# Turning attention probabilities with VectorE and a trip through DRAM instead of TensorE transposes

## Chip, core and metric

The kernel runs on one core of one Trainium2 chip. The metric is device time in microseconds (us) of one execution. Before the change the median of three runs is 538.23 us (538.05 to 538.24).

## What is computed

One layer of a decoder block for 256 tokens of 1024 features, in float32. A SwiGLU feed-forward network with 2816 hidden features comes first and another comes last; between them stands a mixing layer with two branches, attention with 8 heads of 64 features and a gated linear mixing of positions in chunks of 128 (gMLP). Cut to what matters here:

```python
def reference(x, ...):
    h = x + 0.5 * swiglu(rmsnorm(x, ffn1_norm), ffn1_w_gate, ffn1_w_up, ffn1_w_down)
    n = rmsnorm(h, mix_norm)
    z = n @ w_in                                   # q, k, v and both halves of the gMLP
    attn = moba_attention(q, k, v)                 # 256 tokens are one block: causal softmax attention
    gm = u * (tril(w_s) @ layernorm(v_gmlp) + b_s) # chunks of 128
    gates = sigmoid(n @ w_gate + b_gate)           # 2 x 1024 gates
    merged = gates[:, :D] * (attn @ w_branch_attn) + gates[:, D:] * (gm @ w_branch_gmlp)
    h = h + merged @ w_out
    h = h + 0.5 * swiglu(rmsnorm(h, ffn2_norm), ffn2_w_gate, ffn2_w_up, ffn2_w_down)
    return rmsnorm(h, final_norm)
```

For a head, the softmax gives probabilities with queries along the rows and keys along the columns. The product with the values sums over keys. TensorE sums over partitions, so the probabilities are needed with the keys on the partitions: they have to be transposed.

## The kernel before

**Weights.** All weights pass through one stream of units. A unit is fetched in two halves of 512 KB by the SyncE (SP) queue into one of 7 buffers `raw` (L137), and each half is split into a rounded high part (ScalarE, ACT, L212) and a remainder (VectorE, DVE, L214) in one of 4 unit buffers `w`; TensorE (PE) multiplies with three products in place of one. A fetch waits until the half that was in its buffer seven halves earlier has been split. In the stretch of the change the units are named `gate` (8), then `ba` and `bg` (the two branch projections, taken in turn), then `out`.

**Order.** PE and SP run in the order in which the code is written. DVE and ACT are ordered by a scheduler, except in blocks that say otherwise. PSUM has eight banks, taken in turn.

**The mixing stage.** After q, k and u (the names `pq`, `pu`) PE computes the scores (`sc`, L586) and the mixing of positions (`mix`, L571). DVE masks the scores and finds maxima, ACT takes exponentials (L601), DVE scales by the reciprocal sums (L604, L606). Probabilities stand in `prob`: 128 queries by 8 heads by 128 keys for the first 128 tokens, and by 256 keys for the second. Meanwhile PE computes 16 blocks of gates, `pgate` (L162 and L167; 24 matmuls each), by the loop at L666. `collect` (L205, L209) takes each out of PSUM; DVE and ACT finish it. With four of the blocks goes `gated`, which finishes the gMLP branch and frees the banks of `mix`.

**The transposes.** Behind block 7 `turn(0)` issues 12 transposes by PE (`pk`, L634 to L636), which ACT and DVE copy out (`pT`, L640, L642). Behind block 10 the products with the values of the first four heads follow (`attend`, names `po`, L651 and L653), and then `turn(2)`, the 12 transposes of the other heads; behind block 13 come the last four heads' products. Their result `ao` is then multiplied with the branch weights (`pb`).

**A transfer of the same kind.** In the second feed-forward network the hidden state is turned in the same way as the change will do it: DVE transposes it in squares of 32 (L715), four DMAs of 256 KB write it to DRAM from 32 partitions each in rows of 1 KB (`hd`, L723), and two DMAs of 512 KB bring it back (`ht`, L727).

Of the kernel before, what the change touches and what calls it, by code (L numbers as in the profile page):

```python
# [10 lines left out]
F32 = mybir.dt.float32  # L11
# [7 lines left out]
P = 128  # L19
D = 1024  # L20
S = 256
NT = S // P
DFF = 2816
KB = D // P
FB = DFF // P
HEADS = 8
HD = 64
# [16 lines left out]
def block_kernel(ctx, tc, t, out):  # L44
    nc = tc.nc
# [4 lines left out]
    act = ctx.enter_context(tc.tile_pool(name="act", bufs=1))  # L50
    tmp = ctx.enter_context(tc.tile_pool(name="tmp", bufs=2))
    small = ctx.enter_context(tc.tile_pool(name="small", bufs=4))
    psum = ctx.enter_context(tc.tile_pool(name="psum", bufs=8, space=PSUM))
    dram = ctx.enter_context(tc.tile_pool(name="dram", bufs=1, space=bass.MemoryType.DRAM))

    def bank(name):
        return psum.tile([P, 512], F32, tag="ps", name=name)
# [3 lines left out]
    h = act.tile([P, KB, S], F32, tag="h", name="h")  # L61
# [15 lines left out]
    ident = consts.tile([P, P], F32, name="ident")  # L77
# [133 lines left out]
    def split(hi, lo, src, later=False):  # L211
        nc.scalar.copy(hi, src)  # L212
        def rest():
            nc.vector.tensor_sub(lo, src, hi.bitcast(F32))  # L214
        return rest if later else rest()

    def alloc_T(name, tags):

        return [act.tile([P, 4, 2, S], F32R, tag=tag, name=f"{name}{c}") for c, tag in enumerate(tags)]
# [170 lines left out]
    def products(i0, nT, name, f, gu=None, ahead=ALONE):  # L390
        if gu is None:
            gu = tmp.tile([P, 2, S], F32, tag="gu", name=f"gu{name}{f}")
        w = unit(i0 + f, ahead)
        ps = [bank(f"{name}{'gu'[i]}{f}") for i in range(2)]
        by_passes([(ps[i], weights_of(w, nT, i)) for i in range(2)])
        for i in range(2):
            collect(gu[:, i, :], ps[i])
        return gu
# [50 lines left out]
    first = act.tile([P, 4, 2, S], F32, tag="nD", name="first")  # L449
# [3 lines left out]
    ps = {(f, i): bank(f"f1_{f}{i}") for f, i in at}  # L453
# [59 lines left out]
    with in_order():  # L513
# [6 lines left out]
        mix_a, mix_b = mixed[:, :FB], mixed[:, FB:]  # L520
        gates = mix_a[:, :2 * KB, :]
        gv = mix_a[:, 2 * KB:2 * KB + 4, :].rearrange("p (j a) t -> p j (a t)", j=NT)
        va = mix_b[:, 0:4, :].rearrange("p (j a) t -> p j (a t)", j=NT)
# [5 lines left out]
        prob = [mix_b[:, 8:12, :].rearrange("p a (b n) -> p (a b) n", b=2), mix_b[:, 12:20, :]]  # L529
# [36 lines left out]
    def spatial(ps, gp):  # L566

        for j in range(NT):
            for a in range(2):
                g = 2 * gp + a  # L570
                nc.tensor.matmul(ps[a * HD:(a + 1) * HD, j * P:(j + 1) * P],  # L571
                                 gv[:, j, g * HD:(g + 1) * HD], wsT[:, g, :], start=True, stop=True)


    for j in range(NT):
        n = (j + 1) * P
        per = 512 // n
        pr = prob[j]
        pr2 = pr.rearrange("p (a two) n -> p a two n", two=2)
        for a0 in range(0, HEADS // 2, per):  # L580

            pair = [bank(f"sc{j}{a0}{two}") for two in range(2)]
            for a in range(per):
                for two in range(2):
                    r = slice(two * HD, (two + 1) * HD)
                    nc.tensor.matmul(pair[two][:, a * n:(a + 1) * n], qT[r, a0 + a, j * P:(j + 1) * P],  # L586
                                     kT[r, a0 + a, :n], start=True, stop=True)
            for two in range(2):
                ps = pair[two].rearrange("p (a n) -> p a n", a=per)
                to = pr2[:, a0:a0 + per, two, :]  # L590
                if j:
                    nc.scalar.copy(to[:, :, :n - P], ps[:, :, :n - P])
                nc.vector.tensor_add(to[:, :, n - P:], ps[:, :, n - P:],
                                     mask[:, None, :].to_broadcast([P, per, P]))
        mx = small.tile([P, HEADS], F32, tag="mx", name=f"mx{j}")
        nc.vector.tensor_reduce(mx, pr, axis=AX.X, op=ALU.max)
        nm = small.tile([P, HEADS], F32, tag="nm", name=f"nm{j}")
        nc.vector.tensor_scalar(nm, mx, -(HD ** -0.5), None, op0=ALU.mult)
        sm = small.tile([P, HEADS], F32, tag="sm", name=f"sm{j}")
        for hd in range(HEADS):  # L600
            nc.scalar.activation(pr[:, hd, :], pr[:, hd, :], AF.Exp, bias=nm[:, hd:hd + 1],  # L601
                                 scale=HD ** -0.5, accum_out=sm[:, hd:hd + 1])
        ri = small.tile([P, HEADS], F32, tag="ri", name=f"ri{j}")
        nc.vector.reciprocal(ri, sm)  # L604
        for hd in range(HEADS):
            nc.vector.tensor_scalar(pr[:, hd, :], pr[:, hd, :], ri[:, hd:hd + 1], None, op0=ALU.mult)  # L606


    mix = []
    for pair in range(2):  # L610
        ps = bank(f"mix{pair}")
        for q in range(2):
            mix.append(ps[:, q * S:(q + 1) * S])
            spatial(mix[-1], 2 * pair + q)

    def gate_block(f):
        gz = tmp.tile([P, S], F32, tag="s", name=f"gz{f}")
        collect(gz, by_weights(f"pgate{f}", mg + f // 2, nT2, f % 2))  # L620
        nc.vector.tensor_mul(gz, gz, rows2)
        nc.scalar.activation(gates[:, f, :], gz, AF.Sigmoid, bias=bgate[:, f:f + 1])

    aoT, gmT = alloc_T("ag", ("nC", "nD"))

    def turn(first):

        hps = range(first, first + 2)
        pk0, pk1 = [bank(f"pk0{hp}") for hp in hps], bank(f"pk1{first}")
        for hp in hps:  # L630
            for a in range(2):
                hd, c1 = 2 * hp + a, (2 * (hp - first) + a) * P
                ps = pk0[hp - first]
                nc.tensor.transpose(ps[:, a * S:a * S + P], prob[0][:, hd, :], ident)  # L634
                nc.tensor.transpose(ps[:, a * S + P:a * S + S], prob[1][:, hd, :P], ident)
                nc.tensor.transpose(pk1[:, c1:c1 + P], prob[1][:, hd, P:], ident)  # L636
        t0 = []
        for hp, ps in zip(hps, pk0):
            t0.append(tmp.tile([P, 512], F32, tag="hg", name=f"pT0{hp}"))
            nc.scalar.copy(t0[-1], ps)  # L640
        t1 = tmp.tile([P, 512], F32, tag="gu", name=f"pT1{first}")
        nc.vector.tensor_copy(t1, pk1)  # L642
        return {hp: (t0[q], t1[:, q * S:(q + 1) * S]) for q, hp in enumerate(hps)}

    def attend(hp, t0, t1):

        po = bank(f"po{hp}")
        for a in range(2):
            hd = 2 * hp + a
            r = slice(a * HD, (a + 1) * HD)  # L650
            nc.tensor.matmul(po[r, :S], va[:, 0, hd * HD:(hd + 1) * HD], t0[:, a * S:(a + 1) * S],  # L651
                             start=True, stop=False)
            nc.tensor.matmul(po[r, P:S], va[:, 1, hd * HD:(hd + 1) * HD], t1[:, a * P:(a + 1) * P],  # L653
                             start=False, stop=True)
        split(aoT[:, hp, 0, :], aoT[:, hp, 1, :], po[:, :S])

    def gated(gp):
        m = tmp.tile([P, NT, P], F32, tag="s", name=f"mixb{gp}")
        nc.vector.tensor_add(m, mix[gp].rearrange("p (j i) -> p j i", j=NT),
                             bs[:, gp:gp + 1, :].to_broadcast([P, NT, P]))  # L660
        m2 = tmp.tile([P, S], F32, tag="us", name=f"gm{gp}")
        nc.vector.tensor_mul(m2, m.rearrange("p j i -> p (j i)"), uT[:, gp, :])
        split(gmT[:, gp, 0, :], gmT[:, gp, 1, :], m2)


    for f in range(2 * KB):  # L666
        gate_block(f)
        if f < 4:
            gated(f)
        if f == 7:  # L670
            turned = turn(0)
        elif f == 10:
            for hp in range(2):
                attend(hp, *turned[hp])
            turned = turn(2)
        elif f == 13:
            for hp in range(2, 4):
                attend(hp, *turned[hp])


    mT = alloc_T("mg", ("nA", "nB"))
    for f in range(KB):
        i = mb + 2 * (f // 4)
        ps = bank(f"pb{f}")
        c = slice(f % 4 * P, (f % 4 + 1) * P)
# [14 lines left out]
    with in_order():  # L700
# [3 lines left out]
        first = act.tile([P, 3, 2, S], F32, tag="nA", name="first2")  # L704
        gu = [products(f2, nT3, "f2", f, first[:, f]) for f in range(2)]
# [11 lines left out]
    hd = dram.tile([S, D], F32, name="hd")  # L717
# [117 lines left out]
```

## Time and profile before

| | |
|---|---|
| median of the runs | 538.23 us |
| the profiled execution: its time, its span | 538.72 us, 536.8 us |
| PE busy (matmul) | 528.8 us, 98% of the span |
| PE weight loads | 463.5 us, 86% |
| DVE busy | 405.9 us, 76% |
| ACT busy | 303.0 us, 56% |
| share of the SP queue's packets on 16 DMA engines | 58.2% |
| mean granted PE clock | 0.996 |

The span runs from the first to the last instruction. The profiled execution is 0.49 us above the median. A row of the timeline has the start in us from the span's start, the duration in us (of the whole row, where it holds several instructions), the engine, line, operation, what is written and read, the shape and the count; in brackets stands idle time before it and what ended that. A row of SPq is the issue of a transfer, not its duration.

### The profile page before, as it was taken

How to read it: one execution, taken by the hardware profiler on the slowest of the kernel's cores; microseconds unless marked ns; L12 is line 12 of the kernel's file. 1: busy time of each engine (PE TensorE's matmuls, PEld its weight loads, DVE VectorE, ACT ScalarE, POOL GpSimd, SP SyncE). 2: the span in 40 equal slices, each digit the busy share in tenths (PEclk: the TensorE clock that was granted, in tenths of full speed). 3: DMA queues.
4: the chain of work that ended last, by engine and by line, in shares of the span. 5: the costliest groups of instructions: out<-in, count | busy, mean ns of one | idle time of the engine just before them, and what ended most of it. 6: DMA issues, size and time to landing. Idle time of an engine off the chain costs nothing.

```text
span 536.8 us, 8141 instructions
## 1 busy us (share of the span) xinstructions
PE 528.8 (98%) x3049; PEld 463.5 (86%) x3049; DVE 405.9 (76%) x682; ACT 303.0 (56%) x534; POOL 17.7 (3%) x23
## 2 busy tenths in 40 slices
PE   8999999999999999999999999999999999999995
PEld 7888888888888888888888998888888888888884
DVE  6799998788443689978897787799898878854324
ACT  7768566565433367447886544476657656553402
POOL 0040000000000001000000000001000000000002
PEclk9999999999999999999999999999999999999998
DMA  8985765657756329764266545259588765565002
GB/s 319 396 286 178 253 224 187 197 195 218 230 170 203 103 86 322 258 210 147 80 196 203 172 135 182 96 174 315 165 268 292 235 197 197 178 214 177 20 1 79
DMA packets 31287, 104.10 MB, mean 194 GB/s; under 512 B 3472, under 2 KB 6032, under 8 KB 31248
## 3 DMA queue, kind: packets, MB, share of 16 engines
q1 hardware_dynamic: 30960, 103.25, 58.2%
q8 instruction: 24, 0.39, 0.3%
q10 hardware_dynamic: 288, 0.33, 0.2%
q14 instruction: 15, 0.12, 0.1%
HBM read 101.47 MB, written 2.10 MB: 193 GB/s over the span
## 4 chain that ended last, share of the span: by engine, by line
PE 97%; DMA 1%; DVE 0%; issue 0%; ACT 0%; POOLq 0%; DVEq 0%; POOL 0%; ACTq 0%
PE acc L162 10%; PE f2u L162 7%; PE f2g L162 7%; PE f1u L162 7%; PE f1g L162 7%; PE pgate L162 6%; PE acc L167 5%; PE f2u L167 4%; PE f2g L167 4%; PE f1u L167 4%; PE f1g L167 4%; PE acch L200 4%; PE acch L198 4%; PE acch L199 4%; PE pgate L167 3%; PE pq L162 3%
## 5 line engine op out<-in xcount | busy, mean ns | idle before, releaser
L214 DVE TENSOR_TENSOR w<-raw,w 128x1024 fp32r<-128x1024 f32 x180 | 219.3, 1238 | 53.4 <-ACT w L212 53.0
L212 ACT CAST w<-raw 128x1024 fp32r<-128x1024 f32 x180 | 181.8, 1057 | 59.3 <-PE acc L167 21.2
L162 PE MATMUL f2g<-n,w 128*128 128x512 f32 x176 | 68.8, 391 | 0.0
L162 PE MATMUL f2u<-n,w 128*128 128x512 f32 x176 | 68.8, 391 | 0.0
L162 PE MATMUL f1g<-n,w 128*128 128x512 f32 x160 | 62.6, 391 | 0.0
L162 PE MATMUL f1u<-n,w 128*128 128x512 f32 x160 | 62.5, 391 | 0.0
L162 PE MATMUL acc<-f1h,w 128*128 128x512 f32 x176 | 43.4, 391 | 0.0
L167 PE MATMUL f2u<-n,w 128*128 128x256 f32 x176 | 43.2, 283 | 0.0
L167 PE MATMUL f2g<-n,w 128*128 128x256 f32 x176 | 43.0, 282 | 0.0
L167 PE MATMUL f1u<-n,w 128*128 128x256 f32 x160 | 39.2, 283 | 0.0
L167 PE MATMUL f1g<-n,w 128*128 128x256 f32 x160 | 39.1, 282 | 0.0
L162 PEld LDWEIGHTS f2u<-n,w 128*128 128x128 f32 x176 | 33.1, 188 | 6.3
L162 PEld LDWEIGHTS f2g<-n,w 128*128 128x128 f32 x176 | 33.1, 188 | 6.1
L162 PEld LDWEIGHTS acc<-f1h,w 128*128 128x128 f32 x176 | 31.9, 188 | 5.8
L162 PEld LDWEIGHTS f1u<-n,w 128*128 128x128 f32 x160 | 30.1, 188 | 5.7
L162 PEld LDWEIGHTS f1g<-n,w 128*128 128x128 f32 x160 | 30.1, 188 | 5.6
L167 PEld LDWEIGHTS f2u<-n,w 128*128 128x128 f32 x176 | 33.7, 191 | 0.9
L167 PEld LDWEIGHTS f2g<-n,w 128*128 128x128 f32 x176 | 33.6, 191 | 0.9
L162 PE MATMUL pgate<-n,w 128*128 128x512 f32 x128 | 33.1, 396 | 0.0
L199 PE MATMUL acch<-w,f2h 128*128 128x512 f32 x84 | 32.7, 389 | 0.0
L200 PE MATMUL acch<-w,f2h 128*128 128x512 f32 x84 | 32.7, 389 | 0.0
L198 PE MATMUL acch<-w,f2h 128*128 128x512 f32 x84 | 32.7, 389 | 0.0
(191 smaller groups left out, 933.0 us busy)
## 6 DMA issues: line engine op xcount, KB each, us to landing
raw<-in_f SPq DMA_DIRECT2D x84, 512.0 KB, 5.1
raw<-in_f1d SPq DMA_DIRECT2D x22, 512.0 KB, 4.4
raw<-in_f2d SPq DMA_DIRECT2D x22, 512.0 KB, 3.9
raw<-in_gate SPq DMA_DIRECT2D x16, 512.0 KB, 4.6
raw<-in_qk SPq DMA_DIRECT2D x8, 512.0 KB, 5.4
raw<-in_out SPq DMA_DIRECT2D x8, 512.0 KB, 4.4
front<-in_first SPq DMA_DIRECT2D x7, 384.0 KB, 5.9
raw<-in_v SPq DMA_DIRECT2D x4, 512.0 KB, 4.5
```

The lines of the kernel that those rows point to most:

```text
L162: nc.tensor.matmul(ps, st, both.rearrange("p two n -> p (two n)"), start=first, stop=last)
L167: nc.tensor.matmul(ps[:, n:], st, both[:, 0, :], start=False, stop=False)
L198: nc.tensor.matmul(ps, sh, mh, start=first, stop=False)
L199: nc.tensor.matmul(ps, sh, ml, start=False, stop=False)
L200: nc.tensor.matmul(ps, sl, mh, start=False, stop=last)
L212: nc.scalar.copy(hi, src)
L214: nc.vector.tensor_sub(lo, src, hi.bitcast(F32))
```

## The change

The probabilities are no longer transposed by PE. When a block of queries has been scaled, DVE transposes it in squares of 32 by 32 into `turned` (4 instructions for the first 128 queries, 8 for the others). Eight DMAs on the SP queue (`to_keys`) write these to DRAM, in rows of 1 KB, so that each key gets its row: four of 128 KB behind gate block 2, four of 256 KB behind block 4. Three more of 512 KB (`by_keys`), behind block 6, bring them back with the keys on the partitions, over the place where the probabilities were. All products with the values follow behind block 10, where only half of them were. The copies out of PSUM fall away, `mix` is written ahead of the softmax in the code, and the attention result has a tile of its own.

```diff
+    turned = []
     for j in range(NT):
...
             nc.vector.tensor_scalar(pr[:, hd, :], pr[:, hd, :], ri[:, hd:hd + 1], None, op0=ALU.mult)
...
+        turned.append(mix_a[:, 2 * KB:2 * KB + 4, :] if j == 0 else
+                      act.tile([P, KB, S], F32, tag="nC", name="turned1"))
+        for kb in range(n // 32):
+            nc.vector.transpose(turned[j][:, kb, :].rearrange("p (h c) -> p h c", c=32),
+                                pr[:, :, kb * 32:(kb + 1) * 32])
...
-    def turn(first):
...
+    on_way = [dram.tile([(j + 1) * P, 4, S], F32, name=f"on_way{j}") for j in range(NT)]
+
+    def to_keys(j):
+        for b in range(4):
+            nc.sync.dma_start(on_way[j][:, b, :].rearrange("(k r) n -> r k n", r=32),
+                              turned[j][32 * b:32 * (b + 1)])
+
+    def by_keys():
+        for j, t0, b0 in ((0, 0, 8), (1, 0, 12), (1, 1, 16)):
+            nc.sync.dma_start(mix_b[:, b0:b0 + 4, :], on_way[j][t0 * P:(t0 + 1) * P])
...
-            nc.tensor.matmul(po[r, :S], va[:, 0, hd * HD:(hd + 1) * HD], t0[:, a * S:(a + 1) * S],
+            nc.tensor.matmul(po[r, :S], va[:, 0, hd * HD:(hd + 1) * HD], mix_b[:, 8:16, c],
                              start=True, stop=False)
-            nc.tensor.matmul(po[r, P:S], va[:, 1, hd * HD:(hd + 1) * HD], t1[:, a * P:(a + 1) * P],
+            nc.tensor.matmul(po[r, P:S], va[:, 1, hd * HD:(hd + 1) * HD], mix_b[:, 16:20, c],
                              start=False, stop=True)
...
-        if f == 7:
-            turned = turn(0)
+        if f in (2, 4):
+            to_keys(f // 2 - 1)
+        elif f == 6:
+            by_keys()
         elif f == 10:
-            for hp in range(2):
-                attend(hp, *turned[hp])
-            turned = turn(2)
-        elif f == 13:
-            for hp in range(2, 4):
-                attend(hp, *turned[hp])
+            aoT, = alloc_T("ao", ("nC",))
+            for hp in range(4):
+                attend(hp)
```

Where this puts the transfers on the SP queue is shown by the order in which it issues them. `raw` is a buffer of fetched weights. Before, around the first half of the first `bg` unit:

```order
L137 DMA raw_0_2687<-in_ba 128x1024
L137 DMA raw_1_2750<-in_ba 128x1024
L137 DMA raw_0_2754<-in_bg 128x1024
L137 DMA raw_1_2805<-in_bg 128x1024
L137 DMA raw_0_2809<-in_ba 128x1024
L137 DMA raw_1_2881<-in_ba 128x1024
```

After the change, the same place:

```order
L137 DMA raw_0_2701<-in_ba 128x1024
L641 DMA on_way_2623<-mixed 32x4x256 x4
L137 DMA raw_1_2768<-in_ba 128x1024
L137 DMA raw_0_2772<-in_bg 128x1024
L641 DMA on_way_2624<-turned_2613 32x8x256 x4
L137 DMA raw_1_2827<-in_bg 128x1024
L137 DMA raw_0_2831<-in_ba 128x1024
L648 DMA mixed<-on_way_2623 128x1024
L648 DMA mixed<-on_way_2624 128x1024 x2
L137 DMA raw_1_2885<-in_ba 128x1024
```

The writes of the second block of queries stand right behind the fetch of the first half of `bg`, and the reads right behind the fetch of the first half of the second `ba`. Each of these fetches waits for a split by DVE, of the half that was in its buffer before.

On DVE the transposes stand between the scaling and the next weight splits. Before, from the second scaling on (`pgate` is a gate block in PSUM, `gz` the same in SBUF):

```order
L604 RECIPROCAL ri_2581<-sm_2572 128x8
L606 TENSOR_SCALAR mixed<-mixed,ri_2581 128x256 x8
L209 TENSOR_TENSOR gz_2611<-pgate_2612,lo 128x256
L659 TENSOR_TENSOR mixb_2643<-mix_2591,bs 128x256
L621 TENSOR_TENSOR gz_2611<-gz_2611,rowsb_2163 128x256
L662 TENSOR_TENSOR gm_2645<-mixb_2643,mixed 128x256
L214 TENSOR_TENSOR w_2680<-raw_0_2338,w_2680 128x4x256
```

After:

```order
L624 STREAM_TRANSPOSE mixed<-mixed 128x256 x4
L616 RECIPROCAL ri_2603<-sm_2594 128x8
L618 TENSOR_SCALAR mixed<-mixed,ri_2603 128x256 x8
L209 TENSOR_TENSOR gz_2625<-pgate_2626,lo 128x256
L624 STREAM_TRANSPOSE turned_2613<-mixed 128x256 x8
L632 TENSOR_TENSOR gz_2625<-gz_2625,rowsb_2163 128x256
L664 TENSOR_TENSOR mixb_2657<-mix_2545,bs 128x256
L214 TENSOR_TENSOR w_2694<-raw_0_2338,w_2694 128x4x256
```

The four transposes of the first queries have moved in ahead of the reciprocal of the second, and eight stand ahead of every later split.

More of the change, by code (lines that the diff above doesn't have):

```diff
@@ L594, in block_kernel @@
                                      mask[:, None, :].to_broadcast([P, per, P]))
+    mix = []
+    for pair in range(2):
+        ps = bank(f"mix{pair}")
+        for q in range(2):
+            mix.append(ps[:, q * S:(q + 1) * S])
+            spatial(mix[-1], 2 * pair + q)
+    turned = []
+    for j in range(NT):
+        n, pr = (j + 1) * P, prob[j]
         mx = small.tile([P, HEADS], F32, tag="mx", name=f"mx{j}")
@@ L606, in block_kernel @@
             nc.vector.tensor_scalar(pr[:, hd, :], pr[:, hd, :], ri[:, hd:hd + 1], None, op0=ALU.mult)
[L609 to L614, printed above, removed]
+        turned.append(mix_a[:, 2 * KB:2 * KB + 4, :] if j == 0 else
[3 more added lines that the diff above has]
+                                pr[:, :, kb * 32:(kb + 1) * 32])
     def gate_block(f):
@@ L622, in gate_block, with attend @@
         nc.scalar.activation(gates[:, f, :], gz, AF.Sigmoid, bias=bgate[:, f:f + 1])
-    aoT, gmT = alloc_T("ag", ("nC", "nD"))
-    def turn(first):
[L628 to L645, printed above, removed]
+    gmT, = alloc_T("gm", ("nD",))
+    on_way = [dram.tile([(j + 1) * P, 4, S], F32, name=f"on_way{j}") for j in range(NT)]
[6 more added lines that the diff above has]
+            nc.sync.dma_start(mix_b[:, b0:b0 + 4, :], on_way[j][t0 * P:(t0 + 1) * P])
+    def attend(hp):
         po = bank(f"po{hp}")
@@ L649, in attend @@
             hd = 2 * hp + a
-            r = slice(a * HD, (a + 1) * HD)
-            nc.tensor.matmul(po[r, :S], va[:, 0, hd * HD:(hd + 1) * HD], t0[:, a * S:(a + 1) * S],
+            r, c = slice(a * HD, (a + 1) * HD), slice(hd * 32, (hd + 1) * 32)
+            nc.tensor.matmul(po[r, :S], va[:, 0, hd * HD:(hd + 1) * HD], mix_b[:, 8:16, c],
                              start=True, stop=False)
-            nc.tensor.matmul(po[r, P:S], va[:, 1, hd * HD:(hd + 1) * HD], t1[:, a * P:(a + 1) * P],
+            nc.tensor.matmul(po[r, P:S], va[:, 1, hd * HD:(hd + 1) * HD], mix_b[:, 16:20, c],
                              start=False, stop=True)
```

## Prediction

> **What bounds the kernel now.** I read the page's busy times and its chain first, then the timeline of PE around the transposes, then DVE and SP there, and last the second network, where the same kind of transfer already runs.
>
> ```profile
> PE 528.8 (98%) x3049; PEld 463.5 (86%) x3049; DVE 405.9 (76%) x682; ACT 303.0 (56%) x534; POOL 17.7 (3%) x23
> PE 97%; DMA 1%; DVE 0%; issue 0%; ACT 0%; POOLq 0%; DVEq 0%; POOL 0%; ACTq 0%
> ```
>
> PE is the chain from end to end: 97% of the span. So an instruction taken from PE is a gain of its full spacing, and a wait put before PE is a loss of its full length, wherever it stands. All else is free as long as PE finds its operands.
>
> **What is removed.** PE around the transposes (start, duration; neighbours overlap in the pipeline, so starts are what counts):
>
> ```profile
> 273.51 0.27 PE L634 MATMUL pk<-ident,mixed 128*128 128x128 f32 x1
> ...
> 274.74 1.87 PE L162 MATMUL pgate<-n,w 128*128 128x512 f32 x7
> ...
> 283.29 0.66 PE L651 MATMUL po<-pT,mixed 128*64 128x256 f32 x4
> ...
> 284.79 0.33 PE L634 MATMUL pk<-ident,mixed 128*128 128x128 f32 x1
> ...
> 286.08 1.86 PE L162 MATMUL pgate<-n,w 128*128 128x512 f32 x7
> ```
>
> The first twelve hold PE from 273.51 to 274.74, 1.23 us; the second twelve from 284.79 to 286.08, 1.29 us. Together −2.52 us, all on the path. With the first dozen gone, PE comes to the products with the values at 283.29 − 1.23 = 282.06 instead of 283.29. The products keep their number; moving half of them from block 13 to block 10 costs nothing. They now read runs of 32 numbers instead of one run. No row shows PE doing that, so its price lies between 0 and a doubling of all products (two groups of 284.79 − 283.29 = 1.50 us each, so 3.0). I take 0, by the nearest row: DVE reads the same runs of 32 below at 420 ns, no more than its other instructions of 256 columns.
>
> The copies that fall away (L640 on ACT, L642 on DVE, `pT`) ran beside PE; they give nothing directly.
>
> **What DVE gains in work.** The transposes have the shape of those already in the kernel:
>
> ```profile
> L715 DVE STREAM_TRANSPOSE squares<-h x8: 402/420/442, 370.8 to 386.1; 128x256 f32<-128x256 f32 x8
> 370.77 0.76 DVE L715 STREAM_TRANSPOSE squares<-h 128x256 f32<-128x256 f32 x2
> 260.50 0.20 DVE L604 RECIPROCAL ri<-sm 128x8 f32<-128x8 f32 x1 [2.40 <-ACT mixed L601]
> 260.74 2.19 DVE L606 TENSOR_SCALAR mixed<-mixed,ri 128x256 f32<-128x256 f32 x8
> ...
> 265.31 0.42 DVE L209 TENSOR_TENSOR gz<-pgate,lo 128x256 f32<-128x256 f32 x1
> ...
> 260.00:270.00 10.00, 10.00 (x58) 8.78 (x57) 9.47 (x24) 8.68 (x16) 0.00 (x0) 1.00 0.31 99
> 270.00:280.00 10.00, 10.00 (x65) 8.94 (x64) 10.00 (x23) 8.94 (x18) 0.00 (x0) 1.00 0.61 193
> ```
>
> Two take 0.76, one alone 0.42: each further one adds 0.34 us. The first four (1.36 us) fit into the 2.40 us in which DVE waits for the exponentials before L604, and cost nothing. The other eight, 2.72 us, find no gap: a window row has the stretch, its length, the busy us and count of PE, PE's weight loads, DVE, ACT and POOL, then the granted clock, the share of the DMA engines and GB/s, so DVE is busy for 9.47 of 10 us and then 10.00 of 10 us. So everything on DVE behind them until about 280 comes 2.7 us later. Does that stop PE? Block 7 takes the PSUM bank of block 1, which DVE's L209 frees. It started at 265.31; behind the eight transposes (2.72), and behind a split (1.1) and a small subtraction (0.3) that the new order puts ahead of it, it ends at about 269.9. PE needs the bank when block 7 begins, at 273.51 less one block of 2.8, 270.7. That just holds: 0, bounded by 1 us.
>
> **What SP does, and when.** The order shows that the four writes of the second queries follow the fetch of the first half of `bg`, and the reads the fetch of the first half of the second `ba`. Before, these fetches went out when DVE had finished a split:
>
> ```profile
> 270.92 1.23 DVE L214 TENSOR_TENSOR w<-raw,w 128x1024 fp32r<-128x1024 f32 x1
> 272.20 0.33 SPq L137 DMA_DIRECT2D raw<-in_bg  x1
> 276.52 1.23 DVE L214 TENSOR_TENSOR w<-raw,w 128x1024 fp32r<-128x1024 f32 x1
> 277.81 0.33 SPq L137 DMA_DIRECT2D raw<-in_ba  x1
> ```
>
> 270.92 + 1.23 = 272.15, then the issue at 272.20; the other pair likewise. Both splits come 2.7 us later now, the first 0.3 less, since one small instruction has moved behind it. So the writes start at 272.20 + 2.4 + 0.4 (one issue) = 275.0, though the last transpose ends about 266 (the scaling ends at 260.74 + 2.19 = 262.9, then one instruction and 2.72): SP holds them for 9 us, behind fetches that wait for splits on the same DVE. The reads could start at 277.81 + 2.7 + 0.4 = 280.9. Two of the three read what the second four write, and must wait until it has landed.
>
> How long that takes is shown by the same transfer in the second network:
>
> ```profile
> 386.50 0.33 SPq L723 DMA_DIRECT2D hd<-squares  x1
> 388.23 1.34 SPq L723 DMA_DIRECT2D hd<-squares  x1
> DMA to landing us min/median/max: 2.9/4.2/5.2
> ...
> DMA to landing us min/median/max: 6.5/7.2/7.4
> ...
> 405.57 0.42 SPq L727 DMA_DIRECT2D ht<-hd  x1
> 406.04 0.42 SPq L727 DMA_DIRECT2D ht<-hd  x1
> DMA to landing us min/median/max: 5.5/6.0/6.4
> ```
>
> The first landing row is that of the four writes (L723), the second that of the four weight fetches issued right behind them (L137, from 389.6 on), the third that of the two reads (L727). The last write lands at 388.23 + 5.2 = 393.4, 6.9 us after the first issue. From 275.0 that gives 281.9; the weight fetch issued just ahead is still moving, 512 KB, for which I add 1.2 (the reads land about 1.3 apart: 405.57 + 5.5 = 411.1, 406.04 + 6.4 = 412.4). So the writes have landed at 283.1, bounds 281.9 and 283.1. Then the second read goes out, with two fetches that SP has put ahead of it. It takes 5.5 (a read behind one fetch) to 7.4 us (a fetch behind such writes); I take 6.4, between them, since both conditions hold in part: 289.5, bounds 287.4 and 290.5. The first product of PE needs the first two reads; the second needs the third, 1.3 later, of which 0.3 passes under the first.
>
> PE therefore waits at the products: 289.5 − 282.1 = 7.4 us, then about 1.0 again.
>
> **The clock after such a wait.** PE has no long wait inside the span before. Its start and its end show what one does:
>
> ```profile
> 1.18 3.60 PE L92 MATMUL warm<-zeros 128*128 128x256 bf16 x16 [1.18 <-DVE zeros L89]
> 5.17 2.04 PE L191 MATMUL f<-n,w 128*128 128x256 f32 x8 [0.40 <-ACT n L421]
> 7.05 0.52 PE L167 MATMUL f<-n,w 128*128 128x256 f32 x3
> ...
> 530.07 0.28 PE L200 MATMUL endh<-w,f2h 128*128 128x256 f32 x1
> ...
> 532.00:533.00 1.00, 0.00 (x0) 0.00 (x0) 0.56 (x3) 0.42 (x1) 0.54 (x1) 0.84 0.00 0
> 533.00:534.00 1.00, 0.00 (x0) 0.00 (x0) 0.26 (x1) 0.19 (x1) 0.00 (x0) 0.50 0.14 47
> ```
>
> At the start eight matmuls of 256 columns take 2.04 us, 0.25 each, and from 7.05 the same form goes at 0.12. So PE ran at half speed from 1.18 to about 7.1, 5.9 us. At the end the granted clock (the number behind POOL's) falls from 1.00 to 0.50 near 532.7, 2.3 us after the last matmul. A wait of 7.4 us is longer than that, so I expect PE to go on at half speed. How long, no row shows inside the span: bounds are 0 (nothing of the kind) and the start's 5.9 us, which cost 2.9. I take the start's stretch less its 0.4 us pause and less the 1.0 us that PE waits for the third read anyway: (5.9 − 1.4) / 2 = 2.2 us.
>
> [...]
>
> **Sum.** −2.5 (transposes) + 7.4 (wait for the second read) + 1.0 (the third) + 2.2 (half clock) + 0 (products, bank) = +8.1 us. On the profiled execution that is 538.72 + 8.1 = 546.8; the median of the runs is 0.49 lower, and on it I predict 546.3 us. The work behind is pushed back as a whole: the units of `ba` and `bg` are fetched behind the reads, but PE is then late by more than they are.
>
> **Rivals.**
> *The clock stays.* Everything as above without the 2.2: +5.9, 544.1. For it speaks that no such event is seen inside the span, against it both ends of the span.
> *The transfers are slower.* The writes leave 1 KB rows behind which fetches took up to 7.4 us; if all three reads queue behind such fetches one after another, the last lands near 293 and weights come late too: +11 to +13, 549 to 551. Against it: only 0.61 of the DMA engines is used at 270 to 280 and 0.31 before.
> *DVE becomes the bound.* The bank of block 7 comes late: up to 1 us more than the sum, but part of it would come out of the wait at the products, so at most 547.
> *The transfers are hidden, and the kernel is faster.* Then only the −2.5 is left: 535.7. That needs the third read landed by 282.4, so by the rows above the reads issued by about 276 and the writes by 269, three us after the last transpose at 266. It is the place on SP that decides: nothing but the fetches ahead of the writes keeps them from going out then, and those wait for splits that DVE does after 269. I see no way round that in the order, and the wait shrinks by only 1 us for each us that the writes go out earlier than 275.
>
> **How the numbers follow.** Wait and half clock as summed: 0.58. Clock stays: 0.21. Slower transfers: 0.11. DVE: 0.02. Faster: 0.04. Something cancels nearly everything: 0.04. The likeliest is 546.3. For the range: the low end has the writes at 281.9, the read 5.5 later, PE waiting 5.3 and 0.9, no clock loss: +3.7, 541.9. The high end has 290.5, 8.4 and 1.3 of waiting, 2.9 of clock: +10.1, 548.3; slower transfers reach to 551, of which I take in half: 549.8. A change of less than 0.2% (1.1 us) is about what a measurement of this kernel cannot tell from none. Faster by more: 0.04; within: 0.03; slower: 0.93.
>
> **What the profile after would show.** No `pk` rows; twelve STREAM_TRANSPOSE on DVE near 259 and 265 to 268; L641 of the second queries issued near 275, not near 268; `po` waiting for a DMA for 5 to 9 us near 282; then matmuls at twice their spacing and a granted clock below 1 for some slices near 290. Wrong would be: `po` near 282 with no wait (the reads landed early), or `pgate` behind the wait at the usual 0.23 us (the clock stays).

## The result and the profile after

The changed kernel takes 545.62 us (median of four runs, 544.94 to 546.35) against 538.18 us before: a ratio of 1.0139, 95% interval 1.0121 to 1.0156. It is 7.4 us slower; 8.1 us had been predicted. The profiled execution is the slowest of the four, 546.35 us with a span of 544.6 us, so traces are compared by stage below, not by their totals.

The busy times and the chain of the page after:

```profile
PE 528.7 (97%) x3025; PEld 462.3 (85%) x3025; DVE 408.3 (75%) x692; ACT 301.4 (55%) x530; POOL 17.7 (3%) x23
PE 94%; DMA 3%; DVE 0%; SPq 0%; ACT 0%; issue 0%; POOLq 0%; DVEq 0%; POOL 0%; ACTq 0%
```

24 matmuls are gone (3049 to 3025), yet PE's busy time is the same, and 3% of the chain is now DMA, where it was 1%. The timeline of PE shows both:

```profile
281.01 0.39 PE L162 MATMUL pgate<-n,w 128*128 128x512 f32 x1
289.43 1.09 PE L656 MATMUL po<-mixed 128*64 128x256 f32 x2 [8.02 <-DMA mixed<-on_way]
290.61 0.47 PE L658 MATMUL po<-mixed 128*64 128x128 f32 x1
...
295.71 1.90 PE L162 MATMUL pgate<-n,w 128*128 128x512 f32 x7
```

PE stands 8.02 us before the products. Then the products take 289.43 to 295.71, 6.28 us, where two groups of 1.50 us were enough before. The windows there (stretch, length, busy us and count of PE, PEld, DVE, ACT and POOL, granted clock, DMA share, GB/s) show why:

```profile
284.00:285.00 1.00, 0.00 (x0) 0.00 (x0) 1.00 (x3) 0.76 (x3) 0.00 (x0) 1.00 1.04 389
285.00:286.00 1.00, 0.00 (x0) 0.00 (x0) 1.00 (x2) 0.23 (x1) 0.00 (x0) 0.59 1.00 381
286.00:295.00 9.00, 5.47 (x30) 3.91 (x31) 2.50 (x5) 1.50 (x4) 0.00 (x0) 0.50 0.91 366
295.00:296.00 1.00, 1.00 (x6) 0.63 (x4) 0.42 (x1) 0.31 (x2) 0.00 (x0) 0.79 0.01 4
```

The granted clock halves at about 285.2 and is whole again at about 295.4: the means of the windows at 285 (0.59) and at 295 (0.79) place the two edges. Nearly all products run at half speed. The DMA engines are close to fully busy until then (0.91 to 1.04). On SP and in the chain:

```profile
274.21 3.81 SPq L641 DMA_DIRECT2D on_way<-turned  x4
278.28 1.11 SPq L137 DMA_DIRECT2D raw<-in_bg  x1
...
280.73 3.06 SPq L648 DMA_DIRECT2D mixed<-on_way  x3
```

```profile
276.20 6.61 DMA on_way<-turned
283.27 7.30 DMA mixed<-on_way
```

The second writes go out behind the fetch of the first half of `bg`, from 274.2 on, and the reads behind two further fetches. The last write has landed at 276.20 + 6.61 = 282.8. Only then do the second and third read go out, and the third lands at 283.27 + 7.30 = 290.6. DVE did as foreseen:

```profile
257.56 1.42 DVE L624 STREAM_TRANSPOSE mixed<-mixed 128x256 f32<-128x256 f32 x4
259.84 0.20 DVE L616 RECIPROCAL ri<-sm 128x8 f32<-128x8 f32 x1 [0.85 <-ACT mixed L613]
...
262.52 2.71 DVE L624 STREAM_TRANSPOSE turned<-mixed 128x256 f32<-128x256 f32 x8
```

The first four transposes lie in the gap before the reciprocal, which shrinks from 2.40 to 0.85 us; the last ends at 265.2.

### The profile page after: what moved, and what is told of

Its sections match the earlier page's. It is cut to its first block, busy times and chain, and to the rows that moved or that the text cites. A ratio compares the mean times of both kernels' runs of the same rounds, so it can differ in the third digit from the quotient of the medians.

```text
span 544.6 us, 8118 instructions
## 1 busy us (share of the span) xinstructions
PE 528.7 (97%) x3025; PEld 462.3 (85%) x3025; DVE 408.3 (75%) x692; ACT 301.4 (55%) x530; POOL 17.7 (3%) x23
## 4 chain that ended last, share of the span: by engine, by line
PE 94%; DMA 3%; DVE 0%; SPq 0%; ACT 0%; issue 0%; POOLq 0%; DVEq 0%; POOL 0%; ACTq 0%
PE acc L162 10%; PE f2u L162 7%; PE f2g L162 7%; PE f1u L162 7%; PE f1g L162 7%; PE acc L167 5%; PE pgate L162 4%; PE f2u L167 4%; PE f2g L167 4%; PE f1u L167 4%; PE f1g L167 4%; PE acch L200 4%; PE acch L198 4%; PE acch L199 3%; PE pq L162 3%; PE pgate L167 2%
```

## The experiments

The theory to be tested has two parts: PE waits because of where the writes and reads stand on SP's queue, and the slow products are the clock. The rivals are that such transfers are slow wherever they stand, and that PE is slow on the strided operand. All times below are medians; before took 538.1 to 538.4 us beside each of them.

**All transfers early.**

```diff
-        if f in (2, 4):
-            to_keys(f // 2 - 1)
-        elif f == 6:
+        if f == 0:
+            to_keys(0)
+            to_keys(1)
+        elif f == 2:
             by_keys()
```

> Both groups of writes stand behind gate block 0 and the three reads behind block 2, so that no fetch that waits for a split stands ahead of the second writes; the products stay behind block 10. Theory (the wait comes from the place of the second writes on SP): the second writes go out at about 265.5 to 267.5, right after the last transpose, and have landed 6 to 7 us later, near 273; the reads land near 278 to 281; PE comes to the products at about 281.5 and does not wait, the clock stays at 1.00, each pair of heads takes its 1.5 us, and only the 24 matmuls are left of the difference to before: -2.5 us, 535.7 us (535.0 to 536.5). Rival (transfers of this kind are slow wherever they stand, or starve the weight fetches): a wait of 3 us or more at the products or at a weight unit, 539 us or more. Rival (PE is slow on runs of 32 columns): no wait, but the products take 6 us instead of 3, 538.5 to 539.

534.97 us (534.69 to 537.12), ratio 0.9938 (0.9922 to 0.9955). PE in its trace, whose stages lie 2.4 us later than in the changed kernel since its start was slow (of that below):

```profile
283.37 0.39 PE L162 MATMUL pgate<-n,w 128*128 128x512 f32 x1
283.69 0.66 PE L656 MATMUL po<-mixed 128*64 128x256 f32 x4
...
286.49 1.88 PE L162 MATMUL pgate<-n,w 128*128 128x512 f32 x7
```

No wait, a granted clock of 1.00 from 283 to 287, and both groups of products take 2.80 us. The rival of the strided operand falls. But the reads were not quick:

```profile
L648 SPq DMA_DIRECT2D mixed<-on_way x3: 326/383/647, 273.2 to 274.5; - x3
DMA to landing us min/median/max: 7.3/7.7/8.6
```

The third lands at 274.5 + 8.6 = 283.1, 0.6 us before PE asks. They are early enough, not fast.

**Only the writes early.**

```diff
-        if f in (2, 4):
-            to_keys(f // 2 - 1)
+        if f == 0:
+            to_keys(0)
+            to_keys(1)
         elif f == 6:
             by_keys()
```

> Both groups of writes stand behind gate block 0, the reads stay behind block 6. Theory: the writes have long landed when SP comes to the reads, at about 280.5 to 281.5 behind the fetch of the second ba; nothing is left but the reads' own 5 to 6 us, so the second read lands near 286 to 287 and PE waits 4.5 to 5.5 us and about 1 us for the third; the wait is longer than the 2.3 us after which the clock fell at the end of the span, so half clock follows, 1 to 2.5 us: -2.5 + 5 + 1 + 2, 543.5 us (541.5 to 545). Rival (the place of the writes is all): no wait, 535.7. Rival (the clock falls only behind a wait as long as in the changed kernel): 541.5.

544.71 us (544.25 to 545.93), ratio 1.0125 (1.0109 to 1.0140), which overlaps that of the changed kernel: at most 0.9 us is gained, though the last write goes out at 267.0 instead of 276.2.

```profile
L648 SPq DMA_DIRECT2D mixed<-on_way x3: 423/424/488, 280.2 to 281.2; - x3
DMA to landing us min/median/max: 7.3/8.1/8.9
```

```profile
288.93 1.09 PE L656 MATMUL po<-mixed 128*64 128x256 f32 x2 [7.45 <-DMA mixed<-on_way]
```

No read waits for a write any more, all three go out within 1 us, and yet the second takes 8.1 us instead of 6.4. I had expected 5 to 6. So the wait for the writes is not by itself what costs the time.

**No writes at all.**

```diff
-        if f in (2, 4):
-            to_keys(f // 2 - 1)
-        elif f == 6:
+        if f == 6:
             by_keys()
...
-        for j, t0, b0 in ((0, 0, 8), (1, 0, 12), (1, 1, 16)):
-            nc.sync.dma_start(mix_b[:, b0:b0 + 4, :], on_way[j][t0 * P:(t0 + 1) * P])
+        for u in range(3):
+            nc.sync.dma_start(mix_b[:, 8 + 4 * u:12 + 4 * u, :], t["f2"][u][:, :4, :])
```

> The changed kernel without its eight writes, and with three reads of the same form (128 rows of 4 KB) taken from weights that stand in DRAM from the start instead of from the rows just written; the products get wrong numbers. The reads stay behind block 6. Theory (the reads come late because of their place behind fetches that SP lets go only when splits are done): the reads go out at 280.2 to 281.2 as with early writes, and the second lands no earlier than with early writes by more than 1 us, 287.8 to 288.8; wait 6.5 to 7.5 us and half clock, 543.5 to 544.7 us. Rival (the engines were filled by the writes, or rows just written are read slowly): the fetch ahead lands 3.5 us after its issue, near 283.4, and the reads 1.28 us apart behind it, the second near 286; the wait is 4.7 us and 1 us, 540.5 to 542.5.

545.78 us (545.06 to 546.26), as slow as the changed kernel. The three reads now fetch rows of a weight, so the products are not those of the layer.

```profile
L648 SPq DMA_DIRECT2D mixed<-in_f x3: 424/426/438, 280.0 to 280.9; - x3
DMA to landing us min/median/max: 7.7/8.7/9.5
```

```profile
289.29 1.08 PE L656 MATMUL po<-mixed 128*64 128x256 f32 x2 [8.04 <-DMA mixed<-in_f]
```

The wait is 8.04 us without a single write and with rows that stood in DRAM from the start. That rules out the rival that the writes, or rows just written, make the reads slow. The time is a little above what the theory gave (543.5 to 544.7), since the second read took 8.7 us.

**The reads two fetches earlier.** Writes at 0 as above, and

```diff
-        elif f == 6:
+        elif f == 4:
             by_keys()
```

> Both groups of writes behind gate block 0 as in the run with early writes, the reads behind block 4 instead of 6: two weight fetches fewer stand ahead of them on SP. Theory (the landing is set by the reads' place in the stream of transfers, and transfers land 1.28 us apart once they queue): with early writes the fetch ahead of the new place was issued at 273.9 and landed at 279.05, so the reads go out near 274.3 and land near 280.3, 281.6 and 282.9; PE comes to the products at about 281.3, waits 0.3 us and then about 1 us for the third, and the clock stays: 0.3 + 1.0 - 3.0, 536.5 us (535.0 to 537.2). Rival (these reads take 7 to 9 us from their issue wherever they stand): the third lands near 284, 537.5 to 538.5. Rival (a wait of 1 us already costs the clock): 538 to 539.

538.25 us over ten runs, 536.25 to 541.0: the theory's 536.5 is missed. In the profiled run (the slowest; it lies 2.0 us late from the start) the reads go out at 276.2 to 277.2, 6 to 8 us earlier than in the changed kernel when the start is taken off, and the second takes 7.9 us. The windows of PE (stretch, length, busy, clock, DMA share, GB/s):

```profile
283.00:284.00 1.00, 0.43 (x3) 1.00 1.01 410
284.00:285.00 1.00, 0.24 (x1) 1.00 1.02 414
285.00:286.00 1.00, 0.41 (x4) 1.00 1.04 418
286.00:287.00 1.00, 1.00 (x10) 0.72 1.02 410
...
289.00:290.00 1.00, 1.00 (x9) 0.58 0.80 221
```

PE waits 1.3 and 0.6 us, less than the 2.3 us that I had taken as the point, and the clock falls all the same, from about 286.4 to 289.8. In this execution both rivals are right: the reads take 7 to 9 us, and short waits can cost the clock. For the ten runs the second is not shown. The mean granted clock was 0.993 in this run and in one other; in seven it was 0.997 or more, too high for 3.4 us at half clock, which alone takes 0.003 from the mean of such a run (0.5 × 3.4 of 537 us). Those seven took 536.25 to 538.83 us, so the theory is missed without the clock too. What spreads them is not known, since one execution was traced.

**No fetch under way ahead of the reads.** Writes as in the changed kernel, and the reads right behind the second writes, so that SP lets no fetch go until they are out:

```diff
         if f in (2, 4):
             to_keys(f // 2 - 1)
-        elif f == 6:
-            by_keys()
+            if f == 4:
+                by_keys()
```

> The changed kernel with the reads right behind the second writes, behind block 4 instead of 6: SP waits for the second writes to land with no fetch let go meanwhile, so that nothing but the reads is in flight from then on. Theory (the reads took 6.4 to 8.7 us because of the fetches just ahead of them and behind them): the last write lands near 281, the second read goes out then and lands 3.5 to 5 us later, near 285.5; PE, there at 281.3, waits 3.5 to 4.5 us and about 1 us for the third, and half clock costs 1 to 2.4: -3.0 + 4 + 1 + 2, 542.1 us (541 to 543.5). Rival (these reads take 6.4 us or more whatever is beside them): the second lands at 287.5 to 289.5, 544 to 546 us. Rival (the fetches that SP holds meanwhile come too late for the branch products): a wait at pb besides.

542.52 us (542.14 to 542.94), as the theory said.

```profile
L648 SPq DMA_DIRECT2D mixed<-on_way x3: 338/424/1146, 277.8 to 282.6; - x3
DMA to landing us min/median/max: 3.4/4.5/5.7
```

```profile
285.74 1.08 PE L656 MATMUL po<-mixed 128*64 128x256 f32 x2 [4.33 <-DMA mixed<-on_way]
```

The second read goes out nearly as late as in the changed kernel, at 282.2 instead of 282.9, and lands 3.4 us later instead of 6.4. What differs is what is still under way when it goes out: in the changed kernel two weight fetches and the first read, which land at 285.5, 286.7 and 288.0; here the first read alone, which lands at 283.5. The expectation that nothing but the reads is in flight from then on does not hold to the end: from 284 to 290 the engines moved 2.0 MB (341 GB/s), more than the 1.0 MB of the second and third read. With the two runs before, this shows the cause: the reads are late because weight fetches that went out just ahead of them are still under way on the same DMA engines (from 282.0 to 289.4 their mean share in the changed kernel is 0.96). In the eight other traces of this document in which SP issues the reads, the second read took 6.2 to 8.7 us. What the fetches behind a read add was not tried by itself.

**The products later.** The transfers as changed, `attend` at 14 instead of 10:

```diff
-        elif f == 10:
+        elif f == 14:
```

> The transfers stand as in the changed kernel, the products behind gate block 14 instead of 10, four blocks of 2.8 us later. Theory: the third read lands near 290.6 as in the changed kernel, PE comes to the products near 293 and does not wait; no half clock; the products take 3.0 us: -2.5, 535.7 us (535.0 to 537.0). Rival (the products are slow by their operand of 32-column runs): they take about 6 us without a wait, 538.5 to 539. Rival (the branch products need the attention result too soon behind block 14, or the fetches behind the reads come too late): a wait at the first pb of up to 3 us, 536.5 to 539.

536.03 us (535.91 to 536.2), ratio 0.9960 (0.9945 to 0.9975).

```profile
292.87 0.66 PE L656 MATMUL po<-mixed 128*64 128x256 f32 x4
...
295.67 1.88 PE L162 MATMUL pgate<-n,w 128*128 128x512 f32 x7
...
300.05 0.39 PE L199 MATMUL pb<-ao,w 128*128 128x256 f32 x1 [0.84 <-DVE ao L214]
```

The products take 2.80 us, without a wait. The last rival holds for 0.84 us: the attention result is split too late for `pb`.

**PE kept busy in the wait.**

```diff
         elif f == 10:
+            keep = bank("keep")
+            for i in range(64):
+                nc.tensor.matmul(keep[:, :S], zeros[:, :P], zeros, start=True, stop=True)
```

> The changed kernel with 64 matmuls of 256 bf16 columns on zeros, into a PSUM bank that nothing reads, just ahead of the products: at 0.11 to 0.12 us each they fill 7.0 to 7.7 us, about the whole wait of 8.0 us. They take nothing from the data's way. Theory (what follows the wait is slow because PE's clock fell during it): the second read still lands near 289.3, PE still starts the products there, but the granted clock stays at 1.00 and the products take 3.0 us and the wait for the third read (0.5 to 1.0), not 6.3 us: 543.1 us (542.3 to 543.8), and the runs spread less. Rival (PE is slow on the strided operand, clock or not): nothing changes, 545.5.

543.25 us (542.49 to 543.87), 2.4 us less than the changed kernel with 64 matmuls more. The mean granted clock of the profiled run is 0.996, where the changed kernel's is 0.987, and eight of the products take 0.65 us (290.53 to 291.18) where they took 1.28 there (291.09 to 292.37).

```profile
281.20 7.16 PE L683 MATMUL keep<-zeros 128*128 128x256 bf16 x64
289.07 0.62 PE L656 MATMUL po<-mixed 128*64 128x256 f32 x2 [0.71 <-DMA mixed<-on_way]
290.26 0.32 PE L658 MATMUL po<-mixed 128*64 128x128 f32 x1 [0.57 <-DMA mixed<-on_way]
...
293.01 1.90 PE L162 MATMUL pgate<-n,w 128*128 128x512 f32 x7
```

The second read comes 0.4 us earlier than in the changed kernel; the products take 293.01 − 289.07 = 3.94 us instead of 6.28. The difference, 2.34 us, is the half clock. What is left over the 2.80 us, 1.14, is the wait for the third read. The runs spread as before (1.4 us), which I had expected to shrink.

**DVE's transposes alone.** The kernel before, and in its softmax:

```diff
+        dead = act.tile([P, KB, S], F32, tag="nC", name=f"dead{j}")
+        for kb in range(n // 32):
+            nc.vector.transpose(dead[:, kb, :].rearrange("p (h c) -> p h c", c=32),
+                                pr[:, :, kb * 32:(kb + 1) * 32])
```

> The kernel before, with DVE's twelve transposes added into a tile that nothing reads; PE still turns the probabilities, and no transfer is added. It prices DVE's work by itself. Theory (DVE's 2.7 us delay reaches PE nowhere: PE finds its banks and weights): 538.1 us (537.7 to 538.7). Rival (the bank of block 7 or a split comes late for PE): 0.5 to 2.7 us more, 538.7 to 540.8.

539.44 us (539.19 to 541.0), ratio 1.0030 (1.0018 to 1.0041), 1.3 us more than before: the rival. PE's transposes wait in their middle:

```profile
275.05 0.30 PE L638 MATMUL pk<-ident,mixed 128*128 128x128 f32 x1 [1.31 <-DVE gz L209]
```

The first dozen takes three PSUM banks at once. With DVE 2.7 us late one of them has not been emptied, and this wait of 1.31 us is about the whole difference. In the changed kernel these three banks are not asked for, and no such wait is seen.

**Another queue.** All eleven transfers issued by GpSimd (`nc.gpsimd.dma_start` in place of `nc.sync.dma_start`) in the same places.

> The changed kernel with all its writes and reads issued by GpSimd instead of SyncE, in the same places of the code; GpSimd has nothing else to do there (18 us busy in the whole span), so a write goes out when its transposes are done and a read when the writes have landed, and no fetch of SP stands ahead of either. Theory (the place on SP's queue is what makes them late): writes out at 259 to 262 and 266 to 268, landed by 273; reads landed by 281; no wait, 535.2 us (534.7 to 536.5). Rival (the engines serve the transfers of both queues at once, and weight fetches or reads come late by it): a wait of 1 to 5 us at the products or at a weight, 536.5 to 541. Rival (GpSimd issues such transfers much more slowly than SyncE's 0.3 to 0.4 us): 540 or more.

537.11 us over ten runs (536.66 to 539.4), ratio 0.9978 (0.9965 to 0.9992).

```profile
259.61 2.43 POOL L641 DMA_DIRECT2D on_way<-mixed  x4 [38.90 <-DVE mixed L624]
265.93 2.32 POOL L641 DMA_DIRECT2D on_way<-turned  x4 [3.90 <-DVE turned L624]
268.25 0.59 POOL L648 DMA_DIRECT2D mixed<-on_way  x1
274.88 1.06 POOL L648 DMA_DIRECT2D mixed<-on_way  x2 [6.05 <-ACT w L212]
```

Writes and reads go out as soon as their data is there, as expected. But the second and third read go out only at 274.9 and 275.4, 7.2 us after the last write (267.7). They read what the second writes write, so I put this down to the landing of the last of them, as an estimate (the row names ACT as what ended that wait). The third lands so late that PE waits 0.85 us at its first use. From gate block 0 to `pb` PE takes 49.4 us, 1.6 more than with no wait. It is the rival of shared engines, at its lower end.

**All early, used later.** `to_keys` at 0, `by_keys` at 2, `attend` at 12.

> Writes behind gate block 0 and reads behind block 2, as in the run with all transfers early, but the products behind block 12 instead of 10, which gives the third read 5.6 us more: in that run it landed 0.6 us before PE asked for it. Theory: nothing waits in either, so the time is the same, 535.0 us (534.6 to 535.4), with less spread. Rival (in some runs the third read came late): 0.5 us less than with the products behind block 10. Rival (the split of the attention result now comes too late for the branch products, as with the products behind block 14, 0.8 us there): up to 0.8 us more.

535.02 us (534.75 to 535.32), ratio 0.9943 (0.9930 to 0.9955): 3.1 us faster than before and 10.6 us faster than the change as it was made. No wait stands at the products or at `pb`. It is as fast as with the products behind block 10.

## Why the prediction was right, and where it was not

From the first matmul of gate block 0 to the first of `pb` the trace of before takes 301.82 − 251.02 = 50.80 us, that of after 309.82 − 250.38 = 59.44, so +8.64. The rows before, then after:

```profile
251.02 1.90 PE L162 MATMUL pgate<-n,w 128*128 128x512 f32 x7
...
301.82 0.28 PE L198 MATMUL pb<-ag,w 128*128 128x256 f32 x1
```

```profile
250.38 1.90 PE L162 MATMUL pgate<-n,w 128*128 128x512 f32 x7
...
309.82 0.28 PE L198 MATMUL pb<-ao,w 128*128 128x256 f32 x1
```

The terms:

| term | predicted | measured | from |
|---|---|---|---|
| the 24 transposes, products in one place | −2.5 | −3.0 | the same stretch with no wait (products behind 10 with all early, 12 or 14): 47.83 us |
| wait for the second read | +7.4 | +8.0 | trace after |
| wait for the third | +1.0 | +1.1 | PE kept busy: 3.94 − 2.80 |
| half clock | +2.2 | +2.3 | 6.28 − 3.94 |
| strided operand, bank | 0 | 0 | 2.80 us of products without a wait |
| DVE's work | 0 | 0 here, 1.3 by itself | DVE's transposes alone |

They sum to 8.4 of the 8.64. Two misses, −0.5 and +0.6, nearly cancel, which is luck. The start gives 0.64 back, as the last section tells.

*Transposes.* The direction and place were right. Missed was that the two groups of products, once joined, take 2.80 us instead of 2 × 1.50. The other 0.25 us may lie in PE's changing over from gates to something else once instead of three times; no run shows it by itself.

*The wait.* The chain of the trace is the predicted one: second writes from 274.2 (275.0 predicted), landed 282.8 (283.1), second read 6.4 us later (6.4). But a reason given with it was wrong. The prediction said that the place of the writes decides, and that the wait shrinks by 1 us for each us that they go out earlier. They went out 9 us earlier and the wait shrank by 0.6 us; without any writes it did not shrink. The step that failed is to have taken the 6.4 us as a length of the read's own, to be laid behind whatever released it. With the writes early the second read went out at 280.7 instead of 282.9 and took 8.1 us instead of 6.4; with no fetch ahead it took 3.4. What counts is whether fetches are still under way ahead of the reads, and so the reads' place on SP far more than that of the writes. That the 6.4 was met is luck: it was the middle between two rows of other transfers.

*The clock.* Right in size: 6.0 us from the first product to the end of the half clock, where 5.9 us of the start had been taken as the model. The start was half in pace only: its granted clock reads 1.00 (from 0 to 8 us in the trace of before). Nor is the 2.3 us that I took from the end of the span a fixed length: here the clock fell 3.8 us after PE's last matmul (281.4 to 285.2), and in the run with no fetch ahead of the reads 3.9 us after it (281.4 to 285.3). The half clock lasted 10.2 us here (285.2 to 295.4), 6.8 us in that run (285.3 to 292.1, the end estimated from the pace of the matmuls), and 3.4 us (286.4 to 289.8) in the run with the reads two fetches earlier. In this last run PE had been busy for 0.43, 0.24 and 0.41 of three us, and for the 0.4 us after them, when the clock fell. What decides when it falls and how long it stays low is not shown.

*The bank.* The argument that block 7 gets its bank in time held, but it does not make DVE's delay free in general: the same 2.7 us stopped PE for 1.3 us in the kernel that keeps the `pk` groups. By this comparison the delay was free because the change also removed the group that asks for three banks.

*Of the rivals*, "the clock stays" falls by the run that kept PE busy, "DVE becomes the bound" by the trace, "the transfers are slower" by the third read, which lands at 290.6 and not near 293. "The transfers are hidden" is what moving the calls brings: 535.0 against its 535.7. The prediction saw no way to it in the order as it stands; two numbers in the loop are enough to change that order.

## What to carry to other kernels

A transfer on which the bound engine depends should be placed on its queue ahead of prefetches that are not yet needed, and its landing be read with those ahead of it: a read of 512 KB that took 3.4 us with no fetch under way ahead of it took 6.4 us behind two fetches of the same size in the changed kernel, and 6.2 to 8.7 us in the eight other traces in which SP issues the reads. A wait of PE is priced with the clock behind it, here 2.3 us on 9.1 us of waiting; in one execution the clock fell after less than 2 us of it. The 2.7 us more of DVE cost 1.3 us where the next user takes three banks at once, and no wait was seen where that user is gone, so whether an engine's extra work is free is tried in the kernel that keeps the user.

## What was not expected of the hardware

The pace at the start shifts whole runs. In the trace after, the first eight matmuls take

```profile
5.14 1.28 PE L191 MATMUL f<-n,w 128*128 128x256 f32 x8 [0.36 <-ACT n L421]
```

1.28 us, where they took 2.04 us before, and all behind them, up to gate block 0, is 0.64 us earlier. In the profiled run with all transfers early PE's first matmuls went at half pace for longer (the eight in 2.08 us, the next four in 1.05 instead of 0.64, at a granted clock of 1.00), block 0 began at 252.74 instead of 251.02, and that run took 537.12 us where the other three took 534.69 to 535.22. So the start alone moved the stage by up to 2.4 us between these traces (250.38 to 252.74). That it also makes the spread among the runs of one kernel is likely, but one execution of each was traced.

The engines take 512 KB per 1.28 us when they are full (410 to 418 GB/s in the windows of the reads two fetches earlier), yet a transfer among several did not land in the time that the bytes ahead of it need. In the run without writes nothing moved from 278 to 279; from then to 290.4 the engines moved about 3.4 MB (11.4 us at 295 GB/s), six and a half transfers of 512 KB, while five landed: two fetches and the three reads. The rest went to fetches behind them. How the engines share among transfers in flight was not tried, and stays open.
